# A 512-token hybrid decoder layer: the blocks of the residual stream are transposed into the convolution's tile every 14 units, and two weight sums of the gate stream move to VectorE

## The chip, the cores and the metric

The kernel runs on one core of a Trainium2 chip. The metric is the device time of one execution in microseconds (us); the time before is the median of three runs. A profile of one further execution gives the rows quoted below. PE is the TensorE matmul engine and PEld its weight load, DVE is VectorE, ACT is ScalarE, POOL is GpSimd and SP is SyncE, which here only issues DMAs. Each engine works through its own list of instructions in order.

## The reference

One decoder layer in float32 with 512 tokens and width 2048: a mixing part (a recurrent unit beside 16 RWKV heads), a causal convolution FFN of width 6144, a gated embedding and a final norm. The change touches only the FFN's gate and up projections and what runs beside them:

```python
h = h + jnp.concatenate([out_a, out_b], axis=-1) @ w_o[i]

u = rmsnorm(h, ln_ffn[i])
gate = causal_dwconv(u @ w_gate[i], conv_f_w[i], conv_f_b[i])
h = h + (jax.nn.gelu(gate) * (u @ w_up[i])) @ w_down[i]
```

Here `causal_dwconv` has three taps along the tokens, and the norm's factor is applied behind the matmul, to its output. The residual `h` on the last line is needed once more after the down projection, with tokens on the partitions.

## The kernel before

**The gate stream.** A float32 product is made of three fp32r matmuls: each operand is split into a high half (ACT copies it, L138) and a low half (DVE subtracts, L139), and PE adds high x high, high x low and low x high (L1302 to L1304). The gate and up weights go through 48 columns n of 128 features. For each column the 2 x 2 block product (gate and up, two halves of the inputs, two halves of the tokens) is made by a scheme with seven products instead of eight: the units q5, p1, p4, p6, p7, p2, p3. A unit is 24 matmuls of 128x256. Seven units per column make 336 units, which `gate_order` puts in a row; in the text they are numbered from 0 in the order in which TensorE takes them.

Some units need a sum of weight blocks. `gate_unit` (L1126) makes the sums in the tiles x0 to x3 for even n and x4 to x7 for odd n: q5 is the sum of two loaded blocks, p6, p3 and p7 add one more block to a running sum. DVE adds where both blocks have been loaded by SP (L1143); otherwise POOL issues a DMA that adds the block to the tile while it lands (L1160). p6 and p3 take that second way, except p6 of the first and the last column. p2, and p1 and p4 of the first column, are plain loads into the two `wraw` tiles.

The splits of three units ahead are under way while one is multiplied (`LOOK` is 3, three tiles each for high and low halves; every fourth unit has the tiles x12 and x15 of its own). L1208 sets for a few units by how many elements their tile starts later.

**What is made of the outputs.** Two columns n give a tile of 256 outputs, named p = n // 2 in `phase2`. For even n the tile is the gate: it is scaled by the row factors, convolved and put through gelu into the tile x9 (`conv`, L1345, c = B(9)). For odd n it is the up projection, which DVE multiplies with x9 (L1433). After each second p `spill` stores four column sums and differences through the tiles x13 and x14 (rd and dd in HBM).

**The turn.** The 16 blocks of `h` (128 features x 512 tokens) lie in HBM as hd. Each has to be turned: loaded into the tile `row` (called acc in the code), transposed there in squares of 32x32 by DVE in place (L1404), and stored with four DMAs to hx in HBM, in rows of 32 floats (L1407). The code asks for a load (L1414) and four units later a turn, once in 18 units:

```python
m = k // 18 - 1
if 0 <= m < KT and k % 18 == 6:
    nc.sync.dma_start(acc, hd[m // 2][:, m % 2])
if 0 <= m < KT and k % 18 == 10:
    turn(m)
```

**What sets the order.** A scheduler gives each engine its list: it places an instruction as early as its inputs and its tile allow by its own estimate, with priorities from the place in the code. A turn has no input from the stream but `row`, so its place in the code does not hold it there. Before the stream `row` collects the sums of squares of all blocks (L1279), from which the row factors are made: eight matmuls (L202), a small DVE row (L204), a power on POOL (L206), eight matmuls (L215).

Of the kernel before, what the change touches and what calls it, by code (L numbers as in the profile page):

```python
# [13 lines left out]
KT = D // 128  # L14
# [6 lines left out]
NF = FF // 128  # L21
# [69 lines left out]
class Builder:  # L91
# [1039 lines left out]
    def gate_unit(self, n, u):  # L1131
        nc, p, w = self.nc, n // 2, n % 2
        par = 4 * w
        src = lambda i, j: self.A["wgu"][2 * p + i, w, j]
        buf = lambda i: self.t(self.bp, "x%d" % (par + i), (128, 8, 128), bufs=1)

        def load(k, i, j):
            t = buf(k)
            nc.sync.dma_start(t, src(i, j))
            return t  # L1140
        def add(o, a, b):
            with self.tc.high_priority(offset=-W['offw'] if n < 1 else 0):
                nc.vector.tensor_tensor(o, a, b, ALU.add)  # L1143
            return o
        g = self.gw.setdefault(n, {})
        if u == "q5":
            g[21], g[22], g["s"] = load(0, 1, 0), load(1, 1, 1), buf(3)
            return add(g["s"], g[21], g[22])
        if u == "p1":
            g[11] = load(2, 0, 0)  # L1150
            return g[11]
        if u == "p4":
            return g[22]
        if u == "p7":
            if n < 2:
                g[11] = load(2, 0, 0)
            return add(g[21], g[21], g[11])
        if u == "p6" and n in (0, NF - 1):
            return add(g["s"], g["s"], g[11])
        nc.gpsimd.dma_start(g["s"], src(0, 0 if u == "p6" else 1), accum_op=ALU.add)  # L1160
        return g["s"]

# [68 lines left out]
    def phase2(self):  # L1231
        nc, A, k2 = self.nc, self.A, self.k2
        V, SC, G, TE = nc.vector, nc.scalar, nc.gpsimd, nc.tensor
# [5 lines left out]
        acc = self.t(self.cp, "row", (128, S + 2), bufs=1)[:, 0:S]  # L1239
        self.LOOK = 3  # L1240
        hd = [self.dp.tile([128, 2, S], F32, name="hd%d" % i) for i in range(8)]
# [31 lines left out]
        def squares(m):  # L1273
            if m == 0:
                SC.activation(acc, hT[m], AF.Square)
            else:
                sq = self.aux() if m < 8 else self.rsa
                SC.activation(sq, hT[m], AF.Square)
                V.tensor_tensor(acc, acc, sq, ALU.add)  # L1279
# [14 lines left out]
        B = lambda n, shape=(128, 2, S), dt=F32: self.t(self.bp, "x%d" % n, shape, dt, bufs=1)  # L1294
# [50 lines left out]
        def conv(p, z, c):  # L1345
            V.tensor_tensor(z, z, rs.unsqueeze(1).broadcast_to([128, 2, S]), ALU.mult)
            for i in range(2):
                f = 2 * p + i
                SC.activation(c[:, i], z[:, i], AF.Identity, scale=self.P("cfw", 2 * NF + f), bias=self.P("cfb", f))
                for w in range(2):  # L1350
                    V.scalar_tensor_tensor(c[:, i, 2 - w:S], z[:, i, 0:S - 2 + w], self.P("cfw", w * NF + f), c[:, i, 2 - w:S], ALU.mult, ALU.add)
            SC.activation(c, c, AF.Gelu_apprx_tanh)
# [48 lines left out]
        hx = [self.dp.tile([S, 512], F32, name="hx%d" % i) for i in range(4)]  # L1401

        def turn(m):
            V.transpose(acc, acc)  # L1404
            for a in range(4):
                f = m % 4 * 128 + 32 * a
                nc.sync.dma_start(hx[m // 4][:, f:f + 32].rearrange("(b i) j -> i b j", i=32),  # L1407
                                  acc[32 * a:32 * a + 32].rearrange("i (b j) -> i b j", j=32))

        raw, c = [], None  # L1410
        for k, (n, u) in enumerate(self.gate_order()):
            m = k // 18 - 1
            if 0 <= m < KT and k % 18 == 6:
                nc.sync.dma_start(acc, hd[m // 2][:, m % 2])  # L1414
            if 0 <= m < KT and k % 18 == 10:
                turn(m)
            for m in late.get((n, u), ()):
                squares(m)
            unit(n, u)
            if n == 1 and u == "p6":  # L1420
                self.rstd_bcast(acc, D, RMS_EPS, k2, rs, rt)
                c = B(9)
                conv(0, o, c)
            if u != "p3":
                continue
            p, o = n // 2, G_.pop(n)["out"]
            if n == 0:
                continue
            if n % 2 == 0:
                c = B(9)  # L1430
                conv(p, o, c)
                continue
            V.tensor_tensor(o, o, c, ALU.mult)  # L1433
            raw.append(o)
            if p % 2 == 1:
                spill(p // 2, raw)
                raw = []
# [222 lines left out]
        for cb in range(4):  # L1660
# [8 lines left out]
            n, w = (8, 512) if cb < 3 else (4, 256)  # L1669
# [18 lines left out]
        with self.tc.manual_schedule(engines={ET.PE, ET.DVE, ET.Activation, ET.Pool}):  # L1688
            for tt in range(4):
                pg = {tt: self.mm()[:, 0:256]}  # L1690
                for u in range(5):
                    if u == len(us):
                        us.append(self.wnext())
                    k = 2 * u if u < 2 else 4 * u - 4
# [91 lines left out]
```

## Time and profile before

| | |
|---|---|
| median of three runs | 2527.17 us (2523.64 to 2529.2) |
| profiled execution | 2528.72 us, span 2526.9 us |
| PE busy | 2473.3 us, 98% of the span |
| DVE busy | 1903.1 us, 75% |
| ACT busy | 1250.0 us, 49% |
| POOL busy | 220.3 us, 9% |
| gate stream, first and last L1302 | 900.8 and 1840.4 us |
| turns (L1404), first and last start | 960.2 and 1200.1 us |
| accumulating loads (L1160) | 94, from issue to landing 5.3 to 9.0 us, median 5.7 |
| waits of PE for DVE's low halves in the stream | 4.1 us (3.7 and 0.4) |
| waits of PE for ACT's high halves in the stream | 5.6 us (3.6 and 2.0) |

A row of the timeline gives the start in us from the span's start, the length, the engine, line, operation and tiles (buffer numbers left out), shapes, and in brackets how long the engine sat idle before and what ended that. A row of the busy time by stretch gives the stretch, its length, for each engine its busy time and the count of its instructions, then the granted TensorE clock, the DMA engines' busy share and GB/s. SPq and POOLq stand for the issuing side of an engine.

### The profile page before, as it was taken

Reading aid. Unit: us, or ns where it says so; the run is one execution under the profiler, and the core shown is the slowest. Engines: PE = TensorE matmul, PEld = TensorE weight load, DVE = VectorE, ACT = ScalarE, POOL = GpSimd, SP = SyncE. Lnnn points to the kernel's source line nnn. Section 1 sums busy time; section 2 is a strip of 40 time slices with the busy share of each in tenths; the row PEclk is TensorE's granted clock in tenths of the full one; section 3 lists DMA queues with packets and bytes.
Section 4 is the critical chain, followed back from the end, with each engine's and each line's share of the span. In section 5 each row is a group of like instructions: output and inputs, shape, how many; then the busy total and the mean of one; then the engine's idle time right before and its main releaser. Section 6 shows DMA issues by size and latency. Waiting matters only on the chain.

```text
span 2526.9 us, 51719 instructions
## 1 busy us (share of the span) xinstructions
PE 2473.3 (98%) x21858; PEld 2182.3 (86%) x21858; DVE 1903.1 (75%) x2626; ACT 1250.0 (49%) x1735; POOL 220.3 (9%) x244
## 2 busy tenths in 40 slices
PE   9989999999999989999999999999999999999997
PEld 8867777777777889999999999999988888888887
DVE  5855775776585879878988888888877787896457
ACT  6563654556442545434444444444466454535345
POOL 0000100101031000000000000000000000000001
PEclk9999999999999999999999999999999999999998
DMA  7222222222342568888877777776788686853333
GB/s 260 89 78 63 88 77 65 88 81 68 102 131 93 161 198 218 203 212 221 211 196 176 204 194 193 203 196 176 213 250 234 172 264 188 254 130 117 100 92 109
DMA packets 168570, 402.17 MB, mean 159 GB/s; under 512 B 48529, under 2 KB 60817, under 8 KB 168337
## 3 DMA queue, kind: packets, MB, share of 16 engines
q1 hardware_dynamic: 133744, 307.62, 36.9%
q0 software_dynamic: 19872, 72.36, 17.3%
q10 hardware_dynamic: 14720, 18.88, 2.2%
q8 instruction: 171, 2.80, 0.5%
q14 instruction: 63, 0.51, 0.1%
HBM read 358.16 MB, written 40.63 MB: 158 GB/s over the span
## 4 chain that ended last, share of the span: by engine, by line
PE 60%; DVE 5%; DMA 3%; issue 2%; ACT 1%; POOL 0%; SPq 0%; POOLq 0%; ACTq 0%; DVEq 0%
PE mm L1304 7%; PE mm L1303 7%; PE mm L1302 7%; PE mm L1448 6%; PE mm L1447 6%; PE mm L1451 6%; PE wk L1302 3%; PE wk L1303 3%; PE wk L1304 3%; PE mm L1590 2%; PE mm L1591 2%; PE mm L1592 2%; PE mm L173 2%; PE mm L175 2%; PE mm L177 2%
## 5 line engine op out<-in xcount | busy, mean ns | idle before, releaser
L138 ACT ACTIVATE whi<-x 128x1024 fp32r<-128x1024 f32 x332 | 351.1, 1061 | 450.5 <-PE mm L1303 181.2
L139 DVE TENSOR_TENSOR wlo<-x,whi 128x1024 fp32r<-128x1024 f32 x332 | 404.7, 1219 | 120.4 <-ACT whi L138 116.5
L1302 PE MATMUL mm<-s,whi 128*128 128x256 f32 x1432 | 398.0, 278 | 4.5 <-ACT whi L138 3.6
L1304 PE MATMUL mm<-s,wlo 128*128 128x256 f32 x1432 | 398.3, 278 | 3.8 <-DVE wlo L139 3.7
L1303 PE MATMUL mm<-s,whi 128*128 128x256 f32 x1432 | 397.9, 278 | 0.0
L138 ACT ACTIVATE whi<-wraw 128x1024 fp32r<-128x1024 f32 (+1 forms) x223 | 227.0, 1018 | 341.7 <-PE mm L175 165.3
L139 DVE TENSOR_TENSOR wlo<-wraw,whi 128x1024 fp32r<-128x1024 f32 (+1 forms) x223 | 269.4, 1208 | 132.3 <-ACT whi L138 130.3
L173 PE MATMUL mm<-x,whi 128*128 128x512 f32 x832 | 332.5, 400 | 1.5 <-DVE hT L468 0.9
L177 PE MATMUL mm<-x,wlo 128*128 128x512 f32 x832 | 332.1, 399 | 0.0
L175 PE MATMUL mm<-x,whi 128*128 128x512 f32 x832 | 330.5, 397 | 0.0
L1302 PEld LDWEIGHTS mm<-s,whi 128*128 128x128 f32 x1432 | 270.6, 189 | 5.0 <-ACT whi L138 3.8
L1304 PEld LDWEIGHTS mm<-s,wlo 128*128 128x128 f32 x1432 | 270.0, 189 | 4.7 <-DVE wlo L139 4.7
L1303 PEld LDWEIGHTS mm<-s,whi 128*128 128x128 f32 x1432 | 270.1, 189 | 0.2
L1448 PE MATMUL mm<-whi,s 128*128 128x512 f32 x680 | 265.4, 390 | 0.9 <-DVE s L157 0.9
L1447 PE MATMUL mm<-whi,s 128*128 128x512 f32 x680 | 265.6, 391 | 0.0
L173 PEld LDWEIGHTS mm<-x,whi 128*128 128x128 f32 x832 | 157.1, 189 | 37.1 <-issue 2.7
L177 PEld LDWEIGHTS mm<-x,wlo 128*128 128x128 f32 x832 | 156.9, 189 | 34.0 <-issue 1.9
L175 PEld LDWEIGHTS mm<-x,whi 128*128 128x128 f32 x832 | 157.1, 189 | 33.7 <-issue 1.8
L1451 PE MATMUL mm<-wlo,s 128*128 128x512 f32 x680 | 181.3, 390 | 0.0
L1302 PE MATMUL wk<-s,whi 128*128 128x256 f32 x584 | 162.5, 278 | 2.0 <-ACT whi L138 2.0
L1304 PE MATMUL wk<-s,wlo 128*128 128x256 f32 x584 | 162.4, 278 | 0.4 <-DVE wlo L139 0.4
L1160 POOL DMA_DIRECT2D x<-wgu x94 | 82.7, 880 | 913.5 <-DVE wlo L139 663.9
(579 smaller groups left out, 5386.2 us busy)
## 6 DMA issues: line engine op xcount, KB each, us to landing
x<-wgu SPq DMA_DIRECT2D x144, 512.0 KB, 4.4
x<-wgu POOLq DMA_DIRECT2D x94, 512.0 KB, 5.7
wraw<-wz SPq DMA_DIRECT2D x80, 512.0 KB, 3.5
x<-wd SPq DMA_DIRECT2D x52, 512.0 KB, 6.0
wraw<-wgu SPq DMA_DIRECT2D x51, 512.0 KB, 4.6
x<-wd POOLq DMA_DIRECT2D x44, 512.0 KB, 6.0
wraw<-wpg SPq DMA_DIRECT2D x31, 512.0 KB, 3.5
rd<-x SPq DMA_DIRECT2D x24, 512.0 KB, 4.7
```

Of the source, the lines that this page charges most:

```text
L138: nc.scalar.activation(hi, raw, AF.Copy)
L139: nc.vector.tensor_tensor(lo, raw, hi.bitcast(F32), ALU.subtract)
L173: nc.tensor.matmul(ps, hi[:, k, :], xh, start=first and i == 0, stop=False)
L175: nc.tensor.matmul(ps, hi[:, k, :], xl, start=False, stop=False)
L177: nc.tensor.matmul(ps, lo[:, k, :], xh, start=False, stop=last and i == n - 1)
L1160: nc.gpsimd.dma_start(g["s"], src(0, 0 if u == "p6" else 1), accum_op=ALU.add)
L1302: TE.matmul(ps, wh[:, k, :], xh, start=k == 0, stop=False)
L1303: TE.matmul(ps, wh[:, k, :], xl, start=False, stop=False)
L1304: TE.matmul(ps, wl[:, k, :], xh, start=False, stop=k == 7)
L1447: TE.matmul(ps, x[0][:, k, ts_(tt)], w[0][:, k, :], start=first and k == 0, stop=False)
L1448: TE.matmul(ps, x[1][:, k, ts_(tt)], w[0][:, k, :], start=False, stop=False)
L1451: TE.matmul(ps, x[0][:, k, ts_(tt)], w[1][:, k, :], start=False, stop=last and k == 1)
```

## The change

Two weight sums are made otherwise. p6 of n=1 and p3 of n=0 are added by DVE from blocks that SP has loaded, instead of by an accumulating DMA of POOL; the block that p7 and p6 of n=1 share is loaded at p6, which comes first.

The turn transposes from `row` into the first half of the convolution's tile x9, loads the next block into `row` right behind, and stores from x9. It is called after the up projection of each p from 1 to 16 has been multiplied with x9, which is every 14 units; the first load comes with the first convolution.

```diff
         if u == "p7":
-            if n < 2:
+            if n < 1:
                 g[11] = load(2, 0, 0)
             return add(g[21], g[21], g[11])
-        if u == "p6" and n in (0, NF - 1):
+        if u == "p6" and n in (0, 1, NF - 1):
+            if n == 1:
+                g[11] = load(2, 0, 0)
             return add(g["s"], g["s"], g[11])
+        if u == "p3" and n == 0:
+            return add(g["s"], g["s"], load(1, 0, 1))
         nc.gpsimd.dma_start(g["s"], src(0, 0 if u == "p6" else 1), accum_op=ALU.add)
...
         def turn(m):
-            V.transpose(acc, acc)
+            h = B(9)[:, 0]
+            V.transpose(h, acc)
+            if m + 1 < KT:
+                nc.sync.dma_start(acc, hd[(m + 1) // 2][:, (m + 1) % 2])
             for a in range(4):
                 f = m % 4 * 128 + 32 * a
                 nc.sync.dma_start(hx[m // 4][:, f:f + 32].rearrange("(b i) j -> i b j", i=32),
-                                  acc[32 * a:32 * a + 32].rearrange("i (b j) -> i b j", j=32))
+                                  h[32 * a:32 * a + 32].rearrange("i (b j) -> i b j", j=32))
...
-        for k, (n, u) in enumerate(self.gate_order()):
-            m = k // 18 - 1
-            if 0 <= m < KT and k % 18 == 6:
-                nc.sync.dma_start(acc, hd[m // 2][:, m % 2])
-            if 0 <= m < KT and k % 18 == 10:
-                turn(m)
+        for n, u in self.gate_order():
...
             if n == 1 and u == "p6":
                 self.rstd_bcast(acc, D, RMS_EPS, k2, rs, rt)
+                nc.sync.dma_start(acc, hd[0][:, 0])
                 c = B(9)
                 conv(0, o, c)
...
             raw.append(o)
+            if 0 < p <= KT:
+                turn(p - 1)
```

Three places show how the engines' lists move. The first is POOL at the start of the stream. Before, p3 of n=0 (x3) and p6 of n=1 (x7) are its first accumulating loads, and the power for the row factors (L206) stands behind four of them:

```order
L1160 DMA x3_1570_10859<-wgu 128x1024
L1160 DMA x7_1584_10966<-wgu 128x1024 x2
L1160 DMA x3_1608_11173<-wgu 128x1024
L206 TENSOR_TENSOR rsr_1598_11104<-rsm_1597_11102,mhalf_60 128x4
L1160 DMA x3_1608_11173<-wgu 128x1024
L1160 DMA x7_1636_11411<-wgu 128x1024 x2
```

Now the power is first and the list begins with p3 of n=1:

```order
L206 TENSOR_TENSOR rsr_1600_11108<-rsm_1599_11106,mhalf_60 128x4
L1164 DMA x7_1584_10966<-wgu 128x1024
L1164 DMA x3_1609_11175<-wgu 128x1024 x2
L1164 DMA x7_1637_11414<-wgu 128x1024 x2
L1164 DMA x3_1664_11645<-wgu 128x1024 x2
```

The two accumulating loads have gone, and nothing stands ahead of L206. The second place is DVE, from the split of p6 of n=0 (the row that writes `wlo` from x3) to the low half of p3 of n=0. Before, four rows lie in between, and the last row waits for the accumulating load into x3:

```order
L139 TENSOR_TENSOR wlo_1581_10934<-x3_1570_10859,whi_1580_10933 128x1024
L139 TENSOR_TENSOR wlo_1589_11002<-x5_1583_10964,whi_1588_11001 128x1024
L1279 TENSOR_TENSOR row_1442_10102<-row_1442_10102,rsa_86 128x512
L139 TENSOR_TENSOR x15_1586_10969<-x7_1584_10966,x12_1585_10968 128x1024
L1279 TENSOR_TENSOR row_1442_10102<-row_1442_10102,rsa_86 128x512
L139 TENSOR_TENSOR wlo_1592_11036<-x3_1570_10859,whi_1591_11035 128x1024
```

Now these twelve rows stand from behind the split of q5 of n=1 (x15 from x7) to the same low half, which is the last row; the rows that write x7 from x7 and x6, and x3 from x3 and x1, are the two new sums:

```order
L1283 TENSOR_TENSOR row_1442_10102<-row_1442_10102,rsa_86 128x512
L1143 TENSOR_TENSOR x7_1584_10966<-x7_1584_10966,x6_1595_11070 128x1024
L1333 TENSOR_TENSOR e_1561_10820<-wk_1590_11033,e_1561_10820 128x256
L1283 TENSOR_TENSOR row_1442_10102<-row_1442_10102,rsa_86 128x512
L1334 SCALAR_TENSOR_TENSOR e_1561_10820<-mm_1567_10854,e_1561_10820 128x256
L1336 TENSOR_TENSOR e_1561_10820<-e_1561_10820,wk_1587_11000 128x256
L1283 TENSOR_TENSOR row_1442_10102<-row_1442_10102,rsa_86 128x512
L1337 TENSOR_TENSOR x8_1562_10821<-mm_1567_10854,e_1561_10820 128x512
L139 TENSOR_TENSOR x15_1602_11112<-x4_1582_10962,x12_1601_11111 128x1024
L1143 TENSOR_TENSOR x3_1570_10859<-x3_1570_10859,x1_1591_11034 128x1024
L204 TENSOR_SCALAR rsm_1599_11106<-wk_1598_11101 128x4
L139 TENSOR_TENSOR wlo_1593_11038<-x3_1570_10859,whi_1592_11037 128x1024
```

The two sums stand behind the sums of squares (L1283, before L1279) and the outputs of n=0, and no row of this piece waits for POOL any more. The third place is SP where the turns are issued. Before, around the first spill (rd), stores of the turn (hx), loads of `row` and weight loads alternate, about one turn in six units:

```order
L1414 DMA row_1442_10102<-hd0_10103 128x512
L1139 DMA x6_1698_11946<-wgu 128x1024
L1139 DMA x5_1690_11879<-wgu 128x1024
L1407 DMA hx0_10816<-row_1442_10102 32x16x32 x4
L1139 DMA x4_1689_11877<-wgu 128x1024
L1414 DMA row_1442_10102<-hd1_10104 128x512
L126 DMA wraw_1712_12077<-wgu 128x1024
L1407 DMA hx0_10816<-row_1442_10102 32x16x32 x3
L1139 DMA x2_1725_12177<-wgu 128x1024
L1407 DMA hx0_10816<-row_1442_10102 32x16x32
L1139 DMA x1_1717_12110<-wgu 128x1024
L1414 DMA row_1442_10102<-hd1_10104 128x512
```

Now one load of `row` and four stores from x9 stand behind the store of each p (rd), with the loads of the next weights around them:

```order
L1362 DMA rd1_0_10770<-x10_1704_11981 128x1024
L1139 DMA x0_1772_12573<-wgu 128x1024
L1411 DMA row_1442_10102<-hd1_10104 128x512
L126 DMA wraw_1797_12782<-wgu 128x1024
L1414 DMA hx0_10816<-x9_1737_12273 32x16x32 x4
L1139 DMA x6_1810_12882<-wgu 128x1024
L1139 DMA x5_1802_12815<-wgu 128x1024
L1139 DMA x4_1801_12813<-wgu 128x1024
L126 DMA wraw_1824_13013<-wgu 128x1024
L1139 DMA x2_1837_13113<-wgu 128x1024
L1139 DMA x1_1829_13046<-wgu 128x1024
L1362 DMA rd1_1_10771<-x11_1758_12442 128x1024
```

Between two turns stand ten or so other DMAs where three or four stood. TensorE's list changes only in some 200 matmuls at the start of the stream; behind the stream no engine's list changes.

## The prediction

> **What bounds the kernel now.** I read the page first, then the busy time by stretch for one matmul line, then the rows of each engine around the places where that count falls short.
>
> ```profile
> PE 2473.3 (98%) x21858; PEld 2182.3 (86%) x21858; DVE 1903.1 (75%) x2626; ACT 1250.0 (49%) x1735; POOL 220.3 (9%) x244
> ```
> TensorE counts as busy 98% of the span, so this says little about where it waits: matmuls overlap, and a slow stretch still looks busy. A count of matmuls per time says more. Line L1302 issues every third matmul of the gate stream, and these are five stretches of it (length, busy time and count on PE and on weight load, clock, DMA share, GB/s):
>
> ```profile
> 901.00:952.00 51.00, 31.32 (x106) 21.37 (x105) 0.90 0.70 203
> 952.00:1082.00 130.00, 105.26 (x381) 71.35 (x381) 1.00 0.87 214
> 1082.00:1250.00 168.00, 130.26 (x467) 88.65 (x466) 1.00 0.86 217
> 1250.00:1380.00 130.00, 105.56 (x383) 71.72 (x382) 1.00 0.73 189
> 1380.00:1548.00 168.00, 136.39 (x495) 92.73 (x494) 1.00 0.75 196
> ```
> From 1250 on TensorE makes 495 x 3 matmuls in 168 us, 113 ns each, with nothing waiting: a unit of 24 takes 2.72 us, and there the stream cannot go faster. Against that pace three stretches differ. 1082 to 1250 makes 467 instead of 495: 28 x 3 x 113 ns = **9.5 us lost**. 952 to 1082 makes 381 instead of 383: 0.7 us. 901 to 952 makes 106 where 51 us have room for 150: 44 x 3 x 113 ns = **14.9 us lost**. These 25 us are all that the change can win in this stream; the engine order elsewhere stays as it was.
>
> **The 14.9 us at the start.** The rows of PE, ACT and POOL (start, length, idle time before and what ended it):
>
> ```profile
> 914.69 0.39 PE L1302 MATMUL wk<-s,whi 128*128 128x256 f32 x1 [0.72 <-ACT whi L138]
> 916.43 0.38 PE L1302 MATMUL wk<-s,whi 128*128 128x256 f32 x1 [1.24 <-ACT whi L138]
> ...
> 937.77 0.58 PE L1302 MATMUL mm<-s,whi 128*128 128x256 f32 x1 [3.58 <-ACT whi L138]
> ...
> 939.40 0.58 PE L1304 MATMUL mm<-s,wlo 128*128 128x256 f32 x1 [0.84 <-DVE wlo L139]
> ```
> ```profile
> 919.96 1.08 POOL L1160 DMA_DIRECT2D x<-wgu  x1 [93.57 <-DVE wlo L139]
> 929.19 0.89 POOL L1160 DMA_DIRECT2D x<-wgu  x1 [8.14 <-issue]
> ```
> ```profile
> 929.01 1.06 ACT L138 ACTIVATE whi<-x 128x1024 fp32r<-128x1024 f32 x1 [4.60 <-DMA x<-wgu]
> ...
> 934.76 1.06 ACT L138 ACTIVATE whi<-x 128x1024 fp32r<-128x1024 f32 x1 [4.18 <-DMA x<-wgu]
> 935.73 1.04 ACT L138 ACTIVATE x<-x 128x1024 fp32r<-128x1024 f32 x1
> 936.67 1.04 ACT L138 ACTIVATE whi<-wraw 128x1024 fp32r<-128x1024 f32 x1
> ```
> The two POOL rows are the two accumulating loads that the change takes out: p3 of n=0, then p6 of n=1. The first lands 9 us later (ACT reads it at 929.01), the second only goes out then and lands at 934.7. ACT works in order, so p2 of n=1, whose weights had long been there, gets its high half at 936.67, behind the late p6; and TensorE, which takes p2 before p6, stands from 934 to 937.8 and again until 939.4.
>
> The clock makes it dearer:
>
> ```profile
> 913.60:917.00 3.40, 1.44 (x10) 1.04 (x9) 3.36 (x4) 3.24 (x4) 0.00 (x0) 0.98 0.92 299
> 917.00:920.00 3.00, 3.00 (x16) 3.00 (x16) 2.73 (x3) 0.85 (x2) 0.04 (x1) 0.50 0.91 296
> 934.00:937.40 3.40, 0.19 (x2) 0.00 (x0) 2.74 (x4) 2.63 (x3) 0.00 (x0) 0.99 0.01 1
> 937.40:944.00 6.60, 5.39 (x23) 5.10 (x24) 4.88 (x6) 1.89 (x3) 1.02 (x2) 0.50 0.72 182
> ```
> After each idle stretch the granted clock (third number from the end) is 0.50: 16 matmuls in 917 to 920 and 23 in 937.4 to 944, which is 1.6 and about 2.3 us beyond the 113 ns pace.
>
> **What the change makes of the start.** It adds two DVE sums (L1143) and two 512 KB loads on SP, and takes two issues from POOL. The durations for walking the new order:
>
> ```profile
> 912.27 1.22 DVE L1143 TENSOR_TENSOR x<-x,x 128x1024 f32<-128x1024 f32 x1
> 913.41 0.68 DVE L1279 TENSOR_TENSOR row<-row,rsa 128x512 f32<-128x512 f32 x1
> ...
> 930.10 1.23 DVE L139 TENSOR_TENSOR wlo<-x,whi 128x1024 fp32r<-128x1024 f32 x1 [4.63 <-ACT whi L138]
> ```
> ```profile
> 945.51 2.03 POOL L206 TENSOR_TENSOR rsr<-rsm,mhalf 128x4 f32<-128x4 f32 x1 [0.77 <-DMA wraw<-wgu]
> ```
> Up to 910 nothing moves. Then DVE makes the sum of n=0's p7 ahead of two others (it now ends at about 912.4), ACT has its high half at 913.5, and p7 starts at 913.7 instead of 914.7. It waits once for its low half: one sum, one L1279 and one L139 later, 915.3 instead of 916.4. That wait of 1.35 us is all, so I expect the half clock at 917 to go. At the 113 ns pace p6 of n=0 ends at 923.0, where it ended at 925.9: 2.8 us won. Next, q5 and p4 of n=1 run to 929.7, with a wait of 0.45 us for the last sum of squares and the row-sum matmuls among them:
>
> ```profile
> 944.39 0.79 PE wk L202 x8
> ```
> Now p3 of n=0 comes, and here the new sum is late, because eleven DVE rows stand between p6's low half and it: the sum runs 928.4 to 929.6, the high half comes at 930.7, the low one at 931.9. TensorE stands 1.0 us, then 0.7 (p6's high half), then 0.3 (POOL's 2.03 us power, in whose way two DMA issues no longer stand). From there it runs through: p3, p6, p2 and p7 end at 943.2. The same thirteen units end here in the trace of before:
>
> ```profile
> 951.58 0.28 PE L1304 MATMUL wk<-s,x 128*128 128x256 f32 x1
> ```
> So the walk wins 951.6 - 943.2 = **8.4 us**. Its open cost is the clock: three waits of 2 us in sum between 929.7 and 932 may again bring one stretch of half clock, 1.7 us. The Trainium skill (TensorE: Matmul & The Clock Gate, Why this matters for your kernels) asks for no TensorE gap over about 3 us; by that rule none of the new waits would cost clock and the start would win 8.4. The rows at 914.69 and 916.43 disagree: gaps of 1.0 and 1.5 us were enough for 0.50 at 917. I take the middle between 8.4 and 6.7, **7.5 us**, with 3 to 10 as bounds: 3 if p3's wait grows by a 5.7 us landing (x1's load now waits for the n=0 sum that read it), 10 if DVE's queue runs ahead of the walk.
>
> **The 9.5 us of the turns.** These rows lie in 1082 to 1250 and just ahead:
>
> ```profile
> 1070.75 4.42 DMA hx<-row
> ...
> 1075.31 7.67 DMA row<-hd
> ```
> ```profile
> L1404 DVE STREAM_TRANSPOSE row<-row x16: 702/711/715, 960.2 to 1200.1; 128x512 f32<-128x512 f32 x16
> ```
> ```profile
> 1083.11 0.71 DVE L1404 STREAM_TRANSPOSE row<-row 128x512 f32<-128x512 f32 x1 [5.18 <-DMA row<-hd]
> ...
> 1120.24 0.71 DVE L1404 STREAM_TRANSPOSE row<-row 128x512 f32<-128x512 f32 x1 [4.29 <-issue]
> ```
> ```profile
> 1084.98 0.38 PE L1304 MATMUL mm<-s,wlo 128*128 128x256 f32 x1 [1.80 <-DVE wlo L139]
> ```
> The turn works in place, so the next block's load waits until the four stores have left the row tile (4.4 us), then takes 7.7 us itself, while DVE already stands at the next transpose: 5.2 and 4.3 us idle, with the low halves of the weights queued behind. That is the only place where TensorE starves, and the 16 turns come every 16 us (960.2 to 1200.1), since nothing in the stream holds them. Afterwards TensorE also runs slower without a wait:
>
> ```profile
> 1176.00:1240.00 64.00, 50.92 (x182) 34.80 (x182) 1.00 0.84 202
> 1254.00:1318.00 64.00, 51.98 (x189) 35.37 (x189) 1.00 0.72 184
> ```
> 182 against 189 is 117.2 against 112.9 ns a matmul, 0.10 us a unit. It starts after a wait and ends near 1250, which is where units 116 to 118 have their weights 40 elements further on (L1208); I have no mechanism for it, only that it follows a wait.
>
> In the new code the transpose writes into the convolution's tile and the row tile is refilled at once, 38 us (14 units) ahead of its next use against the 7.7 us above: the DVE wait goes. What is added: 0.71 us of DVE per turn stays as it was, now behind L1433. The cover is that DVE is ahead there:
>
> ```profile
> 1308.56 1.22 DVE L139 TENSOR_TENSOR x<-x,x 128x1024 fp32r<-128x1024 f32 x1 [1.34 <-ACT x L138]
> ...
> 1311.03 1.22 DVE L1433 TENSOR_TENSOR x<-x,x 128x1024 f32<-128x1024 f32 x1
> ```
> ```profile
> 1315.77 0.28 PE L1304 MATMUL wk<-s,x 128*128 128x256 f32 x1
> ```
> The half that DVE finished at 1309.8 is used at 1315.8, 6 us later, and DVE's idle time is spent waiting for ACT. 0.7 us more disappears in that. The new wait is the convolution's: its tile must have been stored before ACT and DVE write it again, seven units (19 us) after the turn. The stores:
>
> ```profile
> x<-wgu SPq DMA_DIRECT2D x144, 512.0 KB, 4.4
> x<-wgu POOLq DMA_DIRECT2D x94, 512.0 KB, 5.7
> ...
> hx<-row SPq DMA_DIRECT2D x64, 64.0 KB, 4.4
> ```
> On SP they stand behind a refill and a weight load that waits for DVE two rows on (some 2 us), need 4 issues of 0.5 us and 4.4 us to land: about 9 us, 10 us of margin. SP's loads behind them are issued 2 to 3 us later. I take **8.5 us** of the 9.5, because DVE's lead after the shorter start is thin: by the walk it is under 0.5 us for units 15 to 18, good for about 1 us of waits. Bounds 0 and 9.5.
>
> **Sum.** 7.5 + 8.5 = 16.0 us. The profiled execution took 2528.72 us (span 2526.9), 1.6 above the median of the three runs shown, so it becomes 2512.7 and the median 2527.2 - 16.0 = **2511 us**.
>
> **Rivals.**
> *The start wins nothing much.* p3's late sum costs as much as the landing it replaces: 3 us there, 8.5 from the turns, 2516 to 2517. For it speaks that DVE was on the chain of waits from 909 to 919; against it, DVE's idle 4.6 us before 930.10, where the new sums fit. Chance 0.12.
> *The slow pace is caught and kept.* One wait of a few tenths at a turn after unit 31 puts TensorE at 117 ns until unit 116 (85 x 0.10 = 8.8 us), one after unit 119 until 228 (11.2 us). Then 2520 to 2523. For it: it happened after several waits from 1082 on. Against: with 5 to 6 us of lead there is no wait. Chance 0.14, half of it on each side of the 0.2% line.
> *Slower.* The place is the turn at odd groups, where spill stores follow at once: stores of turn and spill delay the accumulating load of the next column (median 5.7 us). It decides once that load comes so late that the lead of 5 us is used up, a landing beyond about 11 us. Then 8 turns lose some 1.3 us each and the pace is slow for the 210 units with turns: 10 + 21 = 31 us, 2542. The Trainium skill (DMA: Bandwidth & Descriptors, Specifications) has pieces under 512 B below line rate, and the turn's are 32 floats; the rows of the issues above agree, 64 KB take as long to land as 512 KB. Against it: the turns of before came more than twice as densely, and 952 to 1082 lost only 0.7 us. Chance 0.06.
> *It does not do what it says:* the turns still bunch. The order of the engines has them 14 units apart, so 0.02, 2519.
>
> **How the numbers follow.** Forecast (2506 to 2516) 0.62, the four rivals 0.34, something else within 0.2% 0.04. A measurement of this kernel tells 0.2% (5 us) from no change: faster is below 2522.1. Faster 0.62 + 0.12 + 0.07 + 0.02 = 0.83, of which I leave 0.02 to same; same 0.07 + 0.04 + 0.02 = 0.13; slower 0.06. The range reaches from 2506 (start 10, turns 9.5, plus 2 of run to run) to 2522 (the slow pace once).
>
> **What would show it.** Right: L1302 counts of about 495 per 168 us from 1000 on; no DVE wait for the row tile; p3 of n=0 waiting 1 to 2 us, no half clock after 937; the thirteenth unit ending near 943. Wrong: a DVE or ACT wait for the hx stores; counts near 475 anywhere after 1000; a second stretch of 0.50 clock.

## The result, and the profile after

Timed beside each other, five runs of each: 2516.55 us after (2511.19 to 2518.16) against 2529.2 us before (2523.64 to 2530.92), a ratio of 0.995 with a 95% interval of 0.9934 to 0.9966, that is 8.6 to 16.7 us faster. A second measurement of the unchanged kernel after, with the experiments below, gave 2512.16 us against 2530.84, ratio 0.9929 (0.9914 to 0.9945). The prediction was 2511 us, a gain of 16.0, in a range of 2506 to 2522. The profiled execution after took 2516.55 us, its span is 2514.7.

The first view is again the count of one matmul line per stretch, now L1306 (columns: stretch, length, busy time and count on PE and on its weight load, clock, DMA share, GB/s); the second row is the start of the stream, which begins at 904.7 here:

```profile
904.70:955.70 51.00, 35.90 (x128) 23.81 (x127) 1.00 0.65 205
...
1082.00:1250.00 168.00, 136.28 (x494) 92.56 (x494) 1.00 0.80 210
...
1380.00:1548.00 168.00, 136.28 (x494) 92.61 (x494) 1.00 0.81 212
```

1082 to 1250 now counts 494 like the undisturbed stretch 1380 to 1548, where before it had 467: the loss of the turns is gone to the last matmul. The first 51 us of the stream count 128 where before they counted 106, with a clock of 1.00 instead of 0.90. The turn's own view, and a turn on VectorE's timeline:

```profile
L1409 DVE STREAM_TRANSPOSE x<-row x16: 703/706/708, 994.9 to 1566.7; 128x512 f32<-128x512 f32 x16
...
its engine sat idle before it (us, times) until:
who waited for it (us, times):
```
```profile
1071.17 0.71 DVE L1409 STREAM_TRANSPOSE x<-row 128x512 f32<-128x512 f32 x1
1071.79 0.65 DVE L1366 TENSOR_TENSOR x<-x,x 128x512 f32<-128x512 f32 x1
1072.37 1.22 DVE L139 TENSOR_TENSOR wlo<-wraw,whi 128x1024 fp32r<-128x1024 f32 x1
```

The sixteen turns are spread over 572 us instead of 240, none has idle time before it, and nobody waits for one. At the start of the stream the places of the prediction read so (VectorE, then ScalarE, then the clock by stretch with PE, weight load, DVE, ACT and POOL):

```profile
930.83 1.23 DVE L139 TENSOR_TENSOR x<-x,x 128x1024 fp32r<-128x1024 f32 x1
931.97 1.22 DVE L1143 TENSOR_TENSOR x<-x,x 128x1024 f32<-128x1024 f32 x1
933.10 0.15 DVE L204 TENSOR_SCALAR rsm<-wk 128x4 f32<-128x4 f32 x1
934.31 2.36 DVE L139 TENSOR_TENSOR wlo<-x,whi 128x1024 fp32r<-128x1024 f32 x2 [1.05 <-ACT whi L138]
```
```profile
933.22 2.00 ACT L138 ACTIVATE whi<-x 128x1024 fp32r<-128x1024 f32 x2 [2.43 <-DVE x L1143]
```
```profile
934.33 0.38 PE L1306 MATMUL mm<-s,whi 128*128 128x256 f32 x1 [0.68 <-ACT whi L138]
...
935.28 0.38 PE L1306 MATMUL wk<-s,whi 128*128 128x256 f32 x1 [0.45 <-ACT whi L138]
```
```profile
917.00:920.00 3.00, 1.78 (x15) 1.58 (x15) 3.00 (x4) 1.26 (x2) 0.00 (x0) 1.00 0.08 20
934.00:937.40 3.40, 2.62 (x20) 2.42 (x21) 3.09 (x3) 2.18 (x3) 0.56 (x2) 1.00 0.79 271
937.40:944.00 6.60, 6.47 (x56) 6.27 (x55) 4.84 (x6) 1.06 (x1) 1.00 (x1) 1.00 0.78 160
```

The sum for p3 of n=0 (the row at 931.97) is late, as forecast: ScalarE waits 2.43 us for it and TensorE some 0.7 and 0.45 us. But no stretch of the start has half clock any more.

Where the time went is plainest by units. The table counts the matmuls of the gate stream (the three lines that begin with L1302 before and L1306 after) in groups of 24 from the first and takes differences of their starts, in us:

| | stream begins | units 0 to 13 | 13 to 119 | 119 to 228 | whole stream | span |
|---|---|---|---|---|---|---|
| before | 901.0 | 50.57 | 298.67 | 296.50 | 939.6 | 2526.9 |
| after | 904.7 | 42.90 | 289.22 | 296.48 | 922.5 | 2514.7 |
| after, second profile | 903.6 | 43.03 | 289.22 | 296.48 | 922.6 | 2512.8 |

The stream won 17.1 us: 7.7 in its first thirteen units and 9.4 behind them. The span won only 12.2, because in this execution the part ahead of the stream took 3.7 us longer and the part behind it 1.2 us. Ahead of the stream the program is the same. The stretch 750 to 775 us (columns as above), of before, then of after:

```profile
750.00:775.00 25.00, 24.37 (x508) 18.37 (x506) 15.72 (x30) 6.53 (x11) 5.87 (x3) 1.00 0.43 139
```
```profile
750.00:775.00 25.00, 22.57 (x471) 16.98 (x458) 12.84 (x25) 3.90 (x5) 6.76 (x3) 0.86 0.35 110
```

The clock of 0.86 there is one half-clock stretch of 6.8 us that before does not have. Whether the change brings it was the first thing to find out.

### The profile page after: what moved, and what is told of

The parts are those of the page before. It is cut to its first block, busy times and chain, and to the rows that moved or that the text cites. A ratio compares the mean times of both kernels' runs of the same rounds, so it can differ in the third digit from the quotient of the medians.

```text
span 2514.7 us, 51719 instructions
## 1 busy us (share of the span) xinstructions
PE 2465.0 (98%) x21858; PEld 2174.2 (86%) x21858; DVE 1907.4 (76%) x2628; ACT 1252.3 (50%) x1735; POOL 220.1 (9%) x242
## 4 chain that ended last, share of the span: by engine, by line
PE 66%; DVE 3%; DMA 1%; ACT 1%; issue 1%; POOL 0%; POOLq 0%; ACTq 0%; DVEq 0%
PE mm L1307 8%; PE mm L1308 8%; PE mm L1306 8%; PE mm L1453 6%; PE mm L1452 6%; PE mm L1456 6%; PE wk L1306 3%; PE wk L1307 3%; PE wk L1308 3%; PE mm L1595 2%; PE mm L1597 2%; PE mm L1596 2%; PE mm L173 2%; PE mm L175 2%; PE mm L177 2%
## 5 line engine op out<-in xcount | busy, mean ns | idle before, releaser
L1306 PE MATMUL mm<-s,whi 128*128 128x256 f32 x1432 | 395.8, 277 | 1.4 <-ACT s L156 0.7
L1306 PEld LDWEIGHTS mm<-s,whi 128*128 128x128 f32 x1432 | 268.8, 188 | 1.8 <-ACT s L156 0.9
L1306 PE MATMUL wk<-s,whi 128*128 128x256 f32 x584 | 161.5, 277 | 0.4 <-ACT whi L138 0.4
L1307 PE MATMUL wk<-s,whi 128*128 128x256 f32 x584 | 161.4, 276 | 0.0
```

Of the source, the lines that this page charges most:

```text
L1306: TE.matmul(ps, wh[:, k, :], xh, start=k == 0, stop=False)
L1307: TE.matmul(ps, wh[:, k, :], xl, start=False, stop=False)
```

## The experiments

All runs stand in one table at the end of this section. They answer six questions.

**1. Do the two parts of the change add up?** One kernel has the new turn and the old sums, the other the new sums and the old turn. (The second expectation misstates how often before asks for a turn: it is once in 18 units.)

The first, against after:

```diff
-            if n < 1:
+            if n < 2:
                 g[11] = load(2, 0, 0)
...
-        if u == "p6" and n in (0, 1, NF - 1):
-            if n == 1:
-                g[11] = load(2, 0, 0)
+        if u == "p6" and n in (0, NF - 1):
...
-        if u == "p3" and n == 0:
-            return add(g["s"], g["s"], load(1, 0, 1))
```

The second is before with these same lines turned round.

> The turns every 14 units through the convolution's tile, with the row loaded ahead, but the two sums as before. Theory (the two halves of the change gain apart and add up): the first thirteen units of the gate stream take about 50.6 us as before, with the half clock in their middle; units 13 to 119 take 289 us (before 298.7, after 289.2), 119 to the end 305; the stream about 930 us against 939.6, so the time about 9 us below before, near 2519 to 2520. Rival (most of the gain comes from the sums, and the thin lead of the operands eats the turns' part): 13 to 119 above 294 us and the time above 2523.

> The two sums by VectorE, the turns as before (in the row tile, every seven units twice over, load behind the stores). Theory: the first thirteen units take about 43 us and no half clock lies in them; units 13 to 119 take about 298 us as before, the 5.2 and 4.3 us stands of VectorE at the transposes and the slow pace of 118 ns a matmul being still there; the stream about 932 us, the time about 7 to 8 us below before, near 2521. Rival (with the start in order, VectorE is early enough to hide the stands): 13 to 119 under 293 us and the time near after's 2516.

The turns alone gave 0.9961 (0.9949 to 0.9973) and behind unit 13 did what the theory says: units 13 to 119 took 289.7 us. The first thirteen took 52.4 us instead of the 50.6 expected; why is open. The sums alone gave 0.9989 (0.9976 to 1.0002). The first thirteen units took 42.95 us, the full gain, as the theory has it; but units 13 to 119 took **302.8 us, 4.1 more than before**, which neither reading has. (The three kernels with the old sums and turns lie between 296.3 and 298.7 there.) Its count of L1306 in 952 to 1082, where before has 381, and its transposes, the first three and the group's row:

```profile
952.00:1082.00 130.00, 101.58 (x368) 68.88 (x368) 1.00 0.86 213
```
```profile
930.24 0.71 DVE L1408 STREAM_TRANSPOSE row<-row 128x512 f32<-128x512 f32 x1 [0.70 <-DMA row<-hd]
956.22 0.71 DVE L1408 STREAM_TRANSPOSE row<-row 128x512 f32<-128x512 f32 x1
973.84 0.71 DVE L1408 STREAM_TRANSPOSE row<-row 128x512 f32<-128x512 f32 x1 [2.31 <-DMA row<-hd]
```
```profile
L1408 DVE STREAM_TRANSPOSE row<-row 128x512 f32<-128x512 f32 x16 | 11.4, 711 | 33.3 <-DMA row<-hd 26.9 <-issue 6.3
```

The same row of before:

```profile
L1404 DVE STREAM_TRANSPOSE row<-row 128x512 f32<-128x512 f32 x16 | 11.4, 710 | 30.5 <-DMA row<-hd 16.9 <-issue 9.1 <-DMA x<-wgu 4.5
```

With the start in order, the first turn comes at 930 instead of 960, right behind the waits of the start, and VectorE stands 26.9 us for blocks (last column) instead of 16.9. TensorE's first gap behind unit 13 comes at unit 25, where before had it at unit 61. So the old turns eat half of what the sums win. In the stream the two parts give 7.1 and 3.5 us alone and 17.1 together; of the 6.5 us between, 4.1 are these, 1.9 the longer start of the turns alone, and 0.5 that units 15 to 19 run there at the slow pace of question 5. This rests on one profile of each kernel. By the timed medians it can't be shown: 8.7 and 2.5 us alone stand beside 12.7 and 18.7 together, with intervals of several us.

**2. What of the new turn does it?** It changes three things: the distance (14 units, held there by the tile x9), the second tile, and the load of the next block ahead of the stores. Two kernels keep the distance and give up the others. One loads each block only at its turn, straight into x9:

```diff
             h = B(9)[:, 0]
-            V.transpose(h, acc)
-            if m + 1 < KT:
-                nc.sync.dma_start(acc, hd[(m + 1) // 2][:, (m + 1) % 2])
+            nc.sync.dma_start(h, hd[m // 2][:, m % 2])
+            V.transpose(h, h)
...
-                nc.sync.dma_start(acc, hd[0][:, 0])
```

> The kernel after with the turns at the same 14 units and in the same tile, but each block is loaded right at its turn, straight into the convolution's tile, so VectorE waits for the load. It computes the same. Theory (the distance of the turns does it, since VectorE's lead over the matmuls, 5 to 6 us, is had back within 14 units; the early load is worth little): VectorE stands about 2.5 to 5 us at every turn, units 13 to 119 take 289 to 292 us, the time is within 3 us of after. Rival (the early load does it): the stands reach the matmuls at every turn, 13 to 119 take 295 us or more, the time is 6 us or more above after.

The other turns in place in `row`, loads behind the stores as before, and is held at the distance by a row that adds nothing to the block:

```diff
-        def turn(m):
-            h = B(9)[:, 0]
-            V.transpose(h, acc)
-            if m + 1 < KT:
-                nc.sync.dma_start(acc, hd[(m + 1) // 2][:, (m + 1) % 2])
+        def turn(m, o):
+            h = acc
+            V.scalar_tensor_tensor(acc, o[:, 0], 0.0, acc, ALU.mult, ALU.add)
+            V.transpose(acc, acc)
             for a in range(4):
...
+            if m + 1 < KT:
+                nc.sync.dma_start(acc, hd[(m + 1) // 2][:, (m + 1) % 2])
...
-                turn(p - 1)
+                turn(p - 1, o)
```

> The turns at after's 14 units, but in place in the row tile as before, with the load of the next block behind the four stores; each turn adds, ahead of the transpose, zero times the product of that p to the block (one more VectorE row of about 0.7 us), which is what holds it there. It computes the same. Theory (the distance alone does it; the second tile and the refill ahead of the stores do nothing): the load lands some 12 us after a turn and 26 us ahead of the next, VectorE does not stand at the transposes, units 13 to 119 take 289 to 290 us, the stream 922 to 924 us. Rival (the tile matters: in place, the turn still stands for its stores and load): VectorE idle of a few us at the turns, 13 to 119 above 293 us.

Both have after's stream, 922.4 and 922.3 us. The group row of the transposes, first of the kernel that loads at the turn, then of the one in place:

```profile
L1410 DVE STREAM_TRANSPOSE x<-x 128x512 f32<-128x512 f32 x16 | 11.4, 712 | 25.7 <-DMA x<-hd 25.7
```
```profile
L1410 DVE STREAM_TRANSPOSE row<-row 128x512 f32<-128x512 f32 x16 | 11.2, 702 | 0.0
```

In the first, VectorE stands 25.7 us at its turns, nearly as long as before (its row of before says 30.5), and TensorE does not notice, since each stand, 1.6 us on average and so less than the 2.5 to 5 expected, is had back in the 38 us to the next. So at this distance the early load and the second tile are worth nothing; **the distance is enough by itself**. What x9 does is hold the turn there. What the second tile and the early load would be worth with the turns bunched as before, no run shows.

**3. What was dear about the two accumulating loads?** The prediction described a chain: the second load goes out only when the first has landed. Each of the two sums was given back to POOL alone.

The kernel p3_pool lacks the two lines for p3, the kernel p6_pool has the others as before:

```diff
-        if u == "p3" and n == 0:
-            return add(g["s"], g["s"], load(1, 0, 1))
```
```diff
-            if n < 1:
+            if n < 2:
                 g[11] = load(2, 0, 0)
...
-        if u == "p6" and n in (0, 1, NF - 1):
-            if n == 1:
-                g[11] = load(2, 0, 0)
+        if u == "p6" and n in (0, NF - 1):
```

> The kernel after with the sum for p3 of the first column by the accumulating load of before; the other sum (p6 of n=1) stays with VectorE. Theory (what cost was that the second accumulating load goes out only when the first has landed): with nothing ahead of it p3's load lands by 926 to 929 us from the span's start, p6's sum is there in time, no half clock; the first thirteen units take 42 to 45 us. Rival (each of the two costs its own landing): p3 waits 3 us or more, the thirteen units take 46 us or more.

> The kernel after with the sum for p6 of n=1 by the accumulating load of before; p3 of the first column stays with VectorE. Theory as for the run before: p6's load waits for no other load, goes out when its tile has been read, and lands 5.7 us later; p6 waits 0 to 2 us, the first thirteen units take 43 to 46 us. Rival (each costs its own landing): 3 us of wait and half clock, 47 us or more.

The first thirteen units took 47.55 and 48.74 us, so the rival holds: either load alone costs most of what both cost (50.57). POOL, ACT and PE of the second kernel:

```profile
923.60 1.07 POOL L1162 DMA_DIRECT2D x<-wgu  x1 [96.68 <-DVE x L139]
```
```profile
932.84 1.06 ACT L138 ACTIVATE whi<-x 128x1024 fp32r<-128x1024 f32 x1 [6.16 <-DMA x<-wgu]
```
```profile
935.84 0.58 PE L1304 MATMUL mm<-s,whi 128*128 128x256 f32 x1 [3.32 <-ACT whi L138]
...
938.62 0.58 PE L1306 MATMUL mm<-s,wlo 128*128 128x256 f32 x1 [1.98 <-DVE wlo L139]
```

A single load, with no other ahead of it, goes out at 923.6 and is used at 932.8, 9.2 us later where the median of all such loads is 5.7. ACT stands 6.2 us, everything behind it in its list is late, and PE stands at p2, whose weights were there. With p3's load alone VectorE stands too, and it is p2's low half that is late (DVE and PE of that kernel):

```profile
928.77 1.23 DVE L139 TENSOR_TENSOR wlo<-x,whi 128x1024 fp32r<-128x1024 f32 x1 [3.33 <-ACT whi L138]
```
```profile
937.33 0.58 PE L1306 MATMUL mm<-s,wlo 128*128 128x256 f32 x1 [3.50 <-DVE wlo L139]
```

In both kernels the half clock is back, 6.8 us of it, from 935.4 and 936.2.

**4. Is the longer part ahead of the stream the change's doing?**

> The kernel after, unchanged, profiled and timed once more. In the first profile its gate stream was 17.1 us shorter than before's, but the part ahead of the stream, where the program is the same, was 3.7 us longer, 4.7 of it between 750 and 775 us, where 6.8 us of half clock lay. Theory (that half clock is run to run): the stream begins near 900 us again, its first thirteen units take 42 to 43 us, units 13 to 119 take 289 to 290 us, the span is near 2510 to 2512, and the time of more runs is 14 to 17 us below before. Rival (the change brings it): a start of the stream near 904.5 again and a time about 12 us below before.

Its stream is the same to 0.2 us. It too begins late, at 903.6, but 750 to 775 has clock 1.00, and the longer half clock lies at 153.5 instead, where before has 0.83 (this row is of the second profile of after):

```profile
153.50:163.70 10.20, 9.51 (x51) 7.22 (x52) 4.06 (x6) 6.27 (x11) 0.00 (x0) 0.50 0.15 53
```

Yet one place came back. At one matmul near 763 us TensorE stands 2.19 us in both profiles of after, and 0.57 in before (before, then the two of after):

```profile
762.72 0.73 PE L843 MATMUL wk<-Gm,Tt 32*32 32x16 f32 x64 [0.57 <-DVE Gm L853]
```
```profile
763.57 1.05 PE L843 MATMUL wk<-Gm,Tt 32*32 32x16 f32 x64 [2.19 <-DVE Gm L853]
```
```profile
765.37 0.73 PE L843 MATMUL wk<-Gm,Tt 32*32 32x16 f32 x64 [2.19 <-DVE Gm L853]
```

In the first profile the half clock follows right behind it. The rows lead back to a load into `tmp` from ob that took 5.8 and 5.6 us to land there. In the other twelve profiles it took 3.8 to 4.2, and TensorE stood at most 0.7 us. The program is the same ahead of the stream, and kernels next to after (held_no_refill, spaced_in_place) do not have it. So neither reading holds whole: the half clock lies elsewhere in another execution of the same program, but 1.6 us were lost twice at the same place, and whether that is chance or belongs to this kernel, two profiles can't tell. The other twelve begin the stream between 899.7 and 903.2. Over the five further runs the gain was 18.7 us in the medians (13.9 to 21.8 by the interval), against 12.7 in the first five (8.6 to 16.7); the stream's 17 us lie in the second and just beyond the first.

**5. What is the slow pace?** Before ran many of units 65 to 115 at 2.83 us a unit instead of 2.72, without a wait. The prediction had only seen that it ended where L1208 starts the weight tiles 40 elements later. One kernel takes that shift away, one adds another:

```diff
-        r = [(i, 40 if k // 4 in (3, 5, 7, 29, 57) and k % 4 < 3 else 0) for k, i in enumerate(r)]
+        r = [(i, 40 if k // 4 in (3, 5, 7, 57) and k % 4 < 3 else 0) for k, i in enumerate(r)]
```
```diff
-        r = [(i, 40 if k // 4 in (3, 5, 7, 29, 57) and k % 4 < 3 else 0) for k, i in enumerate(r)]
+        r = [(i, 40 if k // 4 in (3, 5, 7, 25, 29, 57) and k % 4 < 3 else 0) for k, i in enumerate(r)]
```

> The kernel before with one of the five shifted groups of weight tiles taken away (units 116 to 118: their tiles start with the other units' address). Theory (the slow pace of 118 ns a matmul that follows a wait is kept until a unit whose weight tile starts elsewhere): with nothing to end it there, the slow pace goes on from unit 119 to the next shifted group at 228, 109 units at 0.10 us, so 119 to 228 take about 11 us more and the time is near 2538 to 2540. Rival (the pace ends by itself, or by something else near unit 119, the shifted start costs only its own 0.08 us a unit): no change, 2527 to 2530.

> The kernel before with one more shifted group of weight tiles, at units 100 to 102. Before ran units 93 to 115 at the slow pace of 117 to 118 ns. Theory (a unit whose weight tile starts elsewhere ends the slow pace, wherever it stands): units 103 to 115 run at 113 ns, which is 13 x 0.10 = 1.3 us less, while the three shifted units cost what slow ones cost; units 31 to 119 take about 247.7 us instead of 249.05. Rival (the pace ends for another reason near unit 116): 103 to 115 slow as before.

Without the shift the slow pace went on from unit 92 to unit 227, and 119 to 228 took 308.1 us instead of 296.5: **11.6 us lost**, 1.0048 (1.003 to 1.0066). The count of L1302 in that kernel:

```profile
1254.00:1318.00 64.00, 50.91 (x182) 34.01 (x182) 1.00 0.69 177
1480.00:1544.00 64.00, 50.89 (x182) 34.02 (x182) 1.00 0.68 171
1570.00:1634.00 64.00, 51.97 (x189) 35.32 (x189) 1.00 0.73 190
```

Before counts 189 in the first of these stretches. With the shift added at unit 100 nothing can be read: in that execution the slow pace ended with the wait at unit 89 and had not begun again when the shifted units came. It gave 104 to 115 fast, as the theory has it, but 93 to 99 too. So the shifted group at 116 ends the pace (shown by taking it away). It is no rule that every group does: in five profiles (turns_only, held_no_refill, p6_pool and the two of this question) units 15 to 19 run slow, right behind the shifted group at 12 to 14, and are fast again only behind the one at 20 to 22. A wait can end the pace. It need not begin at a wait: in before it begins in units 64 and 92, three units behind the waits in 61 and 89, with a single matmul that starts 184 ns after the last instead of 113. Why is open.

**6. Can the rest of the start be had?** By the count of the first view (128 against 150) after still loses 22 x 3 x 113 ns = 7.5 us there, of which the sixteen matmuls of the row factors (L202, L215) take some 1.7. Three kernels let p3's sum go first, let POOL add the late squares, or do both:

```diff
-            with self.tc.high_priority(offset=-W['offw'] if n < 1 else 0):
+            with self.tc.high_priority(offset=-W['offw'] if n < 1 and u != "p3" else 0):
```
```diff
-                V.tensor_tensor(acc, acc, sq, ALU.add)
+                (V if m < 8 else G).tensor_tensor(acc, acc, sq, ALU.add)
```

> The kernel after with the sum for p3 of the first column given the normal priority, so that VectorE makes it ahead of the sums of squares that stood before it. Theory (p3's sum is late, as the walk had it): the waits of 1.0, 0.8 and 0.6 us in units 8 and 9 of the stream go, the squares and the row-sum matmuls move behind p6 and cost at most half of that there; the first thirteen units take 40 to 41.5 us instead of 42.3 to 42.9, the time is 1 to 2.5 us below after. Rival (VectorE is full there, what is put ahead delays the row factors and the outputs by as much): thirteen units within 0.5 us of after, or longer.

> The kernel after with the eight late sums of squares (blocks 8 to 15) added by POOL, which is idle there, at an estimated 1.75 us each (POOL's adds of this size elsewhere in before's trace), instead of VectorE at 0.68 us. Theory (VectorE's eight rows ahead of p3's sum make it late): p3's waits in units 8 and 9 fall from 2.5 us to under 1 us, the first thirteen units take 40 to 41.5 us, nothing is given back later, the time is 1 to 2 us below after. Rival (the chain of squares becomes late instead, since each is 1.1 us longer and ACT's single tile for the squares waits for POOL): the row factors come late and units 10 to 16 wait, the stream within 1 us of after's 922.5 or longer.

> The run before and, beside it, p3's sum with the normal priority. Alone, that priority won 2.5 us in the first thirteen units and gave it back in units 13 to 15, where the row factors came late behind the squares on VectorE. Theory (with the squares on POOL the two no longer compete): the first thirteen units take 39.5 to 41 us and units 13 to 16 no longer wait, the stream is 919.5 to 921 us, the time 2 us below after. Rival (the squares on POOL are later still): the waits in units 13 to 16 stay at 2.7 us or grow, the stream 922.5 or more.

None wins. With the sum first, the thirteen units took 40.3 us, but part of that is only the border of the count: the eight row-sum matmuls (L202, 1.05 us), which stood in unit 8, now stand in unit 13, with the row factors' eight (L215) behind them. p3's waits are gone, others of the same size come at units 10, 12, 13 and 15, and the stream took 923.0 us; 0.9932 against after's 0.9929. The squares on POOL made it worse, 47.5 us for thirteen units. VectorE, POOL, ScalarE and TensorE there (the first row is the three rows behind it in one):

```profile
910.29 5.65 DVE L1143 TENSOR_TENSOR x<-x,x 128x1024 f32<-128x1024 f32 x3
```
```profile
910.29 1.21 DVE L1143 TENSOR_TENSOR x<-x,x 128x1024 f32<-128x1024 f32 x1
```
```profile
911.42 2.31 DVE L1143 TENSOR_TENSOR x<-x,x 128x1024 f32<-128x1024 f32 x1
```
```profile
913.66 2.28 DVE L1143 TENSOR_TENSOR x<-x,x 128x1024 f32<-128x1024 f32 x1
```
```profile
906.97 3.11 POOL L1283 TENSOR_TENSOR row<-row,rsa 128x512 f32<-128x512 f32 x1 [2.39 <-ACT rsa L1282]
```
```profile
910.82 1.82 POOL L1283 TENSOR_TENSOR row<-row,rsa 128x512 f32<-128x512 f32 x1 [0.74 <-ACT rsa L1282]
913.39 1.47 POOL L1283 TENSOR_TENSOR row<-row,rsa 128x512 f32<-128x512 f32 x1 [0.74 <-ACT rsa L1282]
```
```profile
912.68 0.63 ACT L1282 ACTIVATE rsa<-hT 128x512 f32<-128x512 f32 x1 [1.93 <-POOL row L1283]
...
916.51 0.39 PE L1306 MATMUL wk<-s,whi 128*128 128x256 f32 x1 [3.65 <-ACT whi L138]
```

Three sums of weights take 5.65 us, 1.88 on average instead of 1.22, but they are not alike. The first takes its usual 1.21. The second and the third begin while one of POOL's adds is under way and end 1.1 us after that add has ended (at 912.6 and 914.9), so by these times they wait for it rather than run more slowly. One of POOL's adds takes 3.11; ACT stands for POOL at each square, with p7's high half queued behind; TensorE stands 3.65 us at unit 4. The theory had counted POOL's adds as free because POOL is idle there. With both edits it was the same.

| run | median us (runs) | ratio to before, 95% | units 0 to 13 | 13 to 119 | stream |
|---|---|---|---|---|---|
| after | 2516.55 (5) | 0.9950 (0.9934 to 0.9966) | 42.90 | 289.22 | 922.5 |
| after_again | 2512.16 (5) | 0.9929 (0.9914 to 0.9945) | 43.03 | 289.22 | 922.6 |
| turns_only | 2520.37 (7) | 0.9961 (0.9949 to 0.9973) | 52.43 | 289.74 | 932.5 |
| sums_only | 2526.60 (10) | 0.9989 (0.9976 to 1.0002) | 42.95 | 302.81 | 936.1 |
| held_no_refill | 2512.16 (2) | 0.9927 (0.9904 to 0.9949) | 42.34 | 289.74 | 922.4 |
| spaced_in_place | 2512.19 (3) | 0.9928 (0.9903 to 0.9953) | 42.73 | 289.22 | 922.3 |
| p3_pool | 2517.80 (1) | single run | 47.55 | 289.49 | 927.4 |
| p6_pool | 2520.28 (1) | single run | 48.74 | 289.73 | 928.8 |
| p3_sooner | 2512.15 (6) | 0.9932 (0.9914 to 0.9950) | 40.34 | 292.27 | 923.0 |
| squares_pool | 2515.59 (6) | 0.9941 (0.9923 to 0.9960) | 47.53 | 289.19 | 927.1 |
| squares_p3 | 2517.34 (6) | 0.9948 (0.9928 to 0.9968) | 47.06 | 289.20 | 926.6 |
| before_no_mark | 2542.84 (4) | 1.0048 (1.0030 to 1.0066) | 50.26 | 297.95 | 950.2 |
| before_mark_100 | 2528.46 (1) | single run | 51.09 | 296.27 | 937.7 |

## Why the prediction was right

*The 25 us that can be won, 14.9 at the start and 9.5 at the turns, by counts.* Right as a frame: the stream won 17.1 of them, and behind unit 13 nothing is lost any more.

*Start, 7.5 us.* 7.7 and 7.5 in the two profiles. The walk had the thirteen units end 42.2 us after the stream's beginning; they took 42.9 and 43.0. Its steps held too: p3's sum 27.4 us after the beginning (27.2 measured), then waits of about 1.0, 0.7 and 0.3 (0.8, 0.6 and 0.1, by the same count of starts), p7 waiting once for its low half, 1.35 us (1.4). It left out 0.6 us that are no wait, six of the eight row-factor matmuls:

```profile
941.02 0.83 PE L215 MATMUL wk<-con,rsr 128*128 128x128 f32 x6
```

The stretch of half clock for which the term set 0.9 us aside did not come: the gaps between the stream's matmuls (the row factors' matmuls lie in some) add up to 5.7 us, against 10.5 before, and the longest is 1.4 instead of 3.7. So the walk alone was 0.7 to 0.8 us too good, through these matmuls above all and not through the clock; that 7.5 was met to 0.2 us is in part luck. Nor is the reading firm that the gaps before 914.69 and 916.43 "were enough" for half clock: turns_only, p3_pool and before_mark_100 have the same two gaps, to 0.2 us, and no half clock behind them. The account of what had been dear there did not hold: the prediction had the second accumulating load late because it goes out behind the first, but either load alone costs 4.7 and 5.8 us of the 7.7 (question 3). Taking both out removes the cost under either account.

*Turns, 8.5 of 9.5 us.* 9.4. The term that was mis-sized is the 1 us taken off for VectorE's thin lead in units 15 to 18: no wait came there. The mechanism was right, with one part too many: the prediction named the load behind the stores and the early refill too, and the distance alone does it.

*The slow pace.* The forecast let it go with the waits, and behind unit 13 it went (ahead of it, units 5 to 7, 9 and 10 of the first profile have it, some 0.5 us in all); the rival that it is caught and kept was not met, but its price of 0.10 us a unit and 11.2 us up to unit 228 was right (11.6 measured).

*What the prediction did not see.* It added the two terms as if each stood by itself. Together they do; alone, the sums were worth half in the stream of the one profile, in which the old turns came 30 us sooner. Nor did it price the spread of the part ahead of the stream, 3.7 us in the first profile, beyond "2 of run to run". The first median of 2516.55 lies where the rival "the start wins nothing much" had put the time, and that rival is wrong in every row: a time alone would have confirmed the wrong case.

*Not met:* no engine waits for the hx stores, the odd groups lose nothing, and the turns do stand 14 units apart.

## What to carry to other kernels

Work without a deadline that a scheduler places as early as its tile allows will bunch where the buffers come free; tie it to something that comes by at a steady pace, and its waits can vanish in the lead of the engine, here without an extra buffer or an earlier load. When two edits touch the same engine's lead, time each alone and both together before adding their gains. A DMA that an engine's list runs into costs through all that is queued behind it, so look whose operand is late although its data had long been there.

## What was unexpected of the hardware

- **A pace that stays.** After some waits, and twice after one matmul that starts 0.07 us late, matmuls of 128x256 run at 2.83 us per 24 instead of 2.72, at a granted clock of 1.00, with no wait in between, for 136 units in a row in the kernel without the shift. Units whose weight tile starts 40 elements later cost 2.80 us each themselves and ended it at 20 to 22, 116 to 118 and 228 to 230, but not always at 12 to 14. The cause is open.
- **VectorE and POOL hold each other up.** VectorE's 128x1024 add took 2.31 and 2.28 us instead of 1.21 where it began during one of POOL's adds, and ended 1.1 us after that add. POOL's 128x512 adds took 1.28 to 3.11 us, five of the eight less than the expected 1.75. The Trainium skill (GPSIMD Engine Reference, 1. Specifications) says that GpSimd shares its interfaces to SBUF with VectorE, and that they contend when a VectorE instruction has two inputs there; the rows agree, and give the size.
- **Half clock moves from run to run.** Ahead of the stream, where the program is the same, after met 6.8 us of half clock at 763 us in one profile and 10.2 us at 153 in the next, where before has none and 3.4 us. By the starts of the same matmuls this cost some 3.1 and 2.5 us.
